# Duplicate key halves made on ScalarE and GpSimd, the weight sums of the output product issued earlier, score rows of over 512 keys in two adjoining PSUM banks, in a one-core encoder layer

## The chip, the core and the metric

The kernel runs on one core of a Trainium2 chip. The core has a matrix engine (TensorE: PE for its matmuls, PEld for loading the stationary operand), VectorE (DVE), ScalarE (ACT), GpSimd (POOL) and a sync engine (SP) whose queue issues every transfer of this kernel. Matmuls write to PSUM, eight banks of 512 fp32 columns on 128 partitions; all other tiles are in SBUF. The engines run side by side, each works through its own queue in order, and they wait for one another by semaphores. The metric is the device time of one launch in microseconds (us).

## What is computed

One layer for 1024 prompt positions and 32 sample positions of 1024 features. Everything is fp32; for accuracy each operand of a matmul is split into a rounded high part and a low remainder (`h` and `l` in tile names), and two or three products are summed.

```python
u = rmsnorm(h, g_pre) @ w_in                 # w_in (1024, 4096)
qa, ka, va, ga, qb, kb, vb, gb = split(u)    # 512 columns each, 8 heads x 64
oA = band_attention(qa, ka, va, rel_bias)    # softmax, own 64-frame chunk and the 8 before
oB = stick_breaking(qb, kb, vb)              # strictly causal
y  = concat(oA * silu(ga), oB * silu(gb)) @ w_out
h  = h + rmsnorm(y, g_post)
h  = h + sigmoid(h @ w_ple_gate) * (p @ w_ple)

def stick_breaking(q, k, v, q_pos, k_pos):
    z = einsum(q, k) * ATTN_SCALE
    causal = k_pos < q_pos
    log_beta = log_sigmoid(z)
    log_1m = where(causal, log_sigmoid(-z), 0.0)
    after = reverse_cumsum(log_1m) - log_1m
    w = where(causal, exp(log_beta + after), 0.0)
    return einsum(w, v)
```

The keys and values are outputs as well, and so is the same layer for the sample rows, which attend to caches of 512 earlier positions.

## The kernel before

The program first records all operations with what each reads and writes; `Recorder.order` then lays out the five queues by the hand-kept table of numbers `ORDER` (numbers of recorded operations, one list per engine). `Recorder.emit` issues them from one line, so every instruction of the profile stands at L502, and is told apart by its tiles' names.

**Stages.** In the first 25 us the rows of `x` are loaded, squared on ACT, scaled on DVE (`be<-om,ms,gpre`) and turned on the PE in pieces of 128x128 (`ptx`); ACT writes the high part `hnh` and DVE the low part `hnl`. The matmuls `gpre` spread the norm's weights over the partitions, and the product of `p` and `w_ple` for half of the rows (`ptp`, `php`, `ple`) is made there too. Then the first three column groups of `w_in` are projected (`mm_kA`, `mm_qA`, `mm_vA`, three chunks of 352 rows, 24 matmuls each). After that eight pairs of heads, A and B in turn, go through the attention while `weave` puts the projections of the next pair between their steps; the weights of `w_in` are loaded in halves `wr`, and ACT and POOL split them into `wh` and `wl`. From about 560 us on the output product (`o0P` to `o3P`) and the gate product (`g0P` to `g3P`) run by a scheme of seven products of half-size blocks, which needs sums and differences of the weights' quarters.

**Attention.** `prep_k` makes for each head the high part `kd` (ACT) and the low part `kl` (POOL) of the keys on its 64 partitions, and copies both to the other 64 partitions by a transfer (`kd<-kd`, `kl<-kl`). `scores(i)` makes one row block of 128 queries. Block i sees i+1 blocks of 128 keys, in a band head (A) at most five. With up to 512 keys it takes one PSUM tile with the tag `S`; with more it is cut in two halves, each with a tile, its two matmuls, and its own operations after that: in a B head a sigmoid on ACT and a running product on DVE (`om<-om,SB`), in an A head the custom operation that adds the bias and keeps the running minimum (`om<-SA,biasA`, with a short read of `statA`). POOL then takes differences (B), ACT exponentials (A). The weights are turned (`STREAM_TRANSPOSE`, transfers `swap`, or for the last B rows on the PE, `ptwB`) and split into `wTh` and `wTl`, and `values` multiplies them with the values (`PVA`, `PVB`).

**PSUM.** The banks are given by tags: two for projections, three for `S`, two for turned tiles (`T`), one for `PV`. A tile with a tag waits until all readers of the one that had the bank have ended. `S` also serves `gpre`, and the products of the output stage; `T` also `ptp`, `ptx`, `ptk` (keys of the caches), and in the output stage the copy in PSUM (named `x` and the operand, as in `xS4o`) of each left operand, out of which DVE takes the low part.

**Weight sums.** `sum_weights(w, kt)` loads four quarters (`oB` or `gB`, 256 KB each), makes four sums on POOL in eight instructions, and stores four results. There are four `kt` for the output weights (`o`) and four for the gate's (`g`); `with_sums` puts the eight calls into the attention of pairs 0, 0, 1, 1 (`o`) and 4, 4, 5, 5 (`g`).

Of the kernel before, what the change touches and what calls it, by code (L numbers as in the profile page):

```python
# [13 lines left out]
P = 128  # L14
D = 1024
SEQ = 1024
# [28 lines left out]
0-11 14 12 15 13 16 19-21 18 22-23 17 48-51 26 24 27 25 57 56 54 60 52 61-63 29-30 53 31 28 55 59 66 33-34 32 67 35 58 64-65 37 39 38 36 68 70-71 42-43 41 69 40  # L45
72-77 90-91 45 47 46 44 78-79 92 80-83 93-95 97 99 98 96 120-122 101 100 102-103 123-127 144-149 128-129 106-107 105 130-136 104 109 108 110-111 137-143 150-158
117-118 116 119 168-170 159 114-115 113 112 171-189 199 197 190 198 196 84 160 194 193 192 195 85-86 191 161-167 87 204-205 207 206 88-89 202 200 203 216-222
240-263 201 223-230 214 212 215 213 231-232 210-211 208-209 233-239 288-294 264-287 295-359 362 360 368 370 363-367 372-373 361 369 371 374-376 378-379 392-395
377 380-382 408-409 396 410-411 383 438-439 397-403 384-386 440-441 456-457 387 454-455 388-391 404-407 412-417 426-437 442-453 458-469 472-477 480-491 508-510
470 478 526 511-513 471 479 527 514-517 534-535 550-551 548-549 518-521 558-559 522 560-561 523-524 594-597 525 528-532 610-611 533 536-541 418-425 612-613  # L50
542-547 552-557 562-573 582-583 492-495 584-593 598 496-507 599-600 626-627 601-609 614-625 634-635 628-630 636 676-677 631-633 574-581 637-647 664 690-691 665
698-699 666-669 700-701 670-675 678-682 708-709 683-689 692-697 702-705 744-745 706-707 712-713 710-711 648-651 714-722 652-663 760-761 723 746-747 732-743
748-759 764-767 778-779 768 776-777 769-774 762-763 775 780 724-731 781-783 786-791 800-802 828-835 840-841 854-855 836-839 784-785 842-845 803-805 822-827
846-853 856-861 872-873 862 792-799 863-871 876-887 806-809 896-899 810-821 874-875 908-909 900-907 912-923 928 924-925 929-931 910-911 932-939 942-947 950-952
888-891 953-955 964-966 940-941 967-969 986-987 926-927 988-997 892-895 998-1003 1006-1017 1020-1031 1036-1037 1004-1005 1018-1019 1038-1040 948-949 1041-1046
1032-1033 1047 1034-1035 1052-1053 1048-1049 957 956 958-959 963 960-962 1050-1051 1054-1063 1072 970-973 1073-1076 1108 1077 974-981 1080 982-985 1081
1114-1115 1078-1079 1082-1087 1096-1098 1116-1117 1099-1101 1064-1067 1102-1103 1093 1089 1095 1068-1070 1091 1094 1088 1071 1090 1092 1130-1131 1104 1109-1113
1105-1107 1118-1124 1150-1161 1174-1175 1162-1171 1125-1129 1144-1149 1133 1135 1132 1134 1136 1138 1140 1137 1142 1139 1141 1143 1176-1177 1255 1222-1223 1256
1230-1231 1178-1181 1257-1258 1273-1274 1182-1183 1271-1272 1184 1172-1173 1185-1187 1334-1335 1204-1205 1188-1191 1336-1337 1206-1207 1192-1195 1350-1351
1196-1203 1208-1221 1224-1227 1249 1238-1242 1228 1250 1229 1232 1251-1254 1233-1237 1243-1248 1259 1287 1260-1262 1288 1263-1264 1289-1292 1281-1283 1265  # L60
1352-1353 1266-1268 1293 1269-1270 1275-1280 1284 1294-1296 1430 1297-1299 1374-1375 1382 1431 1300-1301 1383 1285-1286 1302-1313 1322-1323 1328-1332 1438-1439
1333 1452-1453 1338-1339 1324-1325 1454-1455 1326-1327 1340-1349 1354-1359 1462-1463 1360-1361 1314-1320 1367 1321 1366 1362-1365 1368-1373 1376-1378 1390-1395
1412-1429 1379-1381 1384-1386 1492-1493 1387-1389 1464-1471 1480-1481 1432-1437 1440-1446 1396-1399 1447-1450 1516-1517 1451 1456-1458 1494-1495 1459-1460
1400-1411 1461 1482-1491 1504-1506 1532-1533 1507 1472-1479 1518-1519 1497 1496 1498-1499 1501-1502 1500 1503 1508-1515 1520-1531 1546-1548 1552-1554 1549-1551
1564-1565 1555-1558 1602 1559-1560 1603-1606 1561-1563 1566-1569 1607-1608 1573 1572 1574 1535 1537 1577-1578 1534 1536 1575 1579 1576 1570-1571 1580-1585
1609-1613 1539 1541 1543 1545 1538 1540 1542 1544 1635 1641 1586-1589 1614 1636 1615 1590-1592 1628 1593 1629 1594-1596 1620-1621 1597-1601 1634 1632-1633 1631
1630 1642 1616-1619 1622-1625 1657-1658 1626-1627 1637-1640 1643-1645 1667-1668 1646-1648 1669-1672 1649-1656 1673 1661-1666 1682-1687 1708-1709 1718-1719
1688-1689 1659-1660 1690 1674-1681 1691-1693 1702-1704 1740 1705-1707 1712 1724-1725 1741 1713-1715 1710-1711 1716-1717 1720-1722 1694-1697 1723 1728-1730
1698-1700 1731 1760-1761 1742-1743 1762 1701 1763-1767 1726-1727 1768-1771 1732-1739 1744-1749 1788-1793 1802-1803 1794-1799 1804-1813 1816 1832-1833 1817-1821
1826-1830 1834 1831 1835 1814 1800 1815 1801 1836-1837 1842 1750-1751 1872 1843-1846 1873-1874 1847-1848 1838-1839 1822-1825 1754-1756 1753 1752 1759 1758 1757  # L70
1849 1840-1841 1850 1870-1871 1851 1868-1869 1852 1884 1772-1775 1853 1862 1885 1875 1776-1787 1886-1887 1863-1864 1876-1880 1900-1901 1881-1883 1865-1867
1888-1899 1902-1913 1916-1917 1944-1947 1918 1914-1915 1919-1922 1948 1854-1857 1923-1927 1949 1956-1957 1970-1971 1978-1979 1950-1955 1980 1858-1861 1981
1994-1995 1958-1966 1996-1997 1967-1969 1972-1977 1982 2024-2025 1983-1993 1998-2008 2026-2027 2009 2042-2043 2018 2040-2041 2019-2023 2028-2035 2062-2063
2036-2039 2044-2050 1928-1931 2051-2054 2072 2055-2058 2070-2071 2059 2073-2080 1932-1943 2112 2140 2113 2141 2126-2127 2081-2083 2100-2111 2060-2061 2064-2069
2142-2148 2114 2156-2157 2115-2116 2010-2017 2117-2122 2149-2153 2123 2192-2193 2124-2125 2128 2158-2159 2129-2133 2154-2155 2160-2165 2084-2087 2166-2171
2134-2139 2208-2209 2212 2088-2094 2194-2195 2095-2099 2213 2180-2189 2214 2190-2191 2196-2197 2215-2217 2236-2237 2218-2223 2210-2211 2224 2198-2204 2172-2178
2205-2206 2225 2207 2226-2227 2179 2228-2231 2238-2240 2232-2235 2241-2243 2318 2326-2327 2319 2244-2245 2288 2250-2251 2246 2289 2247-2249 2260 2290-2301 2257
2252 2255 2253 2259 2254 2258 2256 2302-2305 2340-2341 2306-2310 2356-2357 2311 2261-2263 2342-2343 2264-2271 2344-2351 2272-2275 2352-2355 2360-2362 2276-2281
2392 2282-2285 2393 2358-2359 2286-2287 2363-2370 2312-2315 2371 2316-2317 2320-2325 2328-2332 2408-2409 2333-2335 2394-2395 2336-2339 2412-2419 2372-2375
2380-2381 2420-2421 2382 2422-2426 2383 2436-2437 2384-2389 2410-2411 2376-2379 2390-2391 2396-2407 2427-2435 2438-2448 2526 2512-2513 2527 2449 2460-2461  # L80
2450-2451 2462-2466 2536 2544-2545 2534 2537 2535 2467-2468 2459 2453-2454 2456 2452 2457-2458 2455 2469-2471 2488 2546-2547 2489-2494 2576 2495-2496 2574-2575
2497 2604-2605 2498-2502 2472-2475 2503-2508 2476-2479 2577 2480 2606-2607 2481-2487 2620-2621 2514-2519 2509-2511 2520-2525 2528-2533 2538-2543 2560-2563 2548
2584 2588 2585-2587 2589 2591 2590 2564-2567 2549-2558 2592-2603 2608-2611 2652-2653 2612-2619 2559 2568-2573 2578-2583 2676-2680 2622 2624 2623 2625 2681 2627
2629 2631 2626 2633 2628 2630 2632 2682-2685 2634-2637 2694-2695 2638-2651 2721 2723 2702 2660 2703 2661-2667 2722 2668-2669 2731-2732 2724 2670 2733-2734
2671-2675 2706 2704-2705 2708 2707 2654-2656 2788-2789 2657 2790-2791 2658-2659 2686-2688 2804-2805 2689-2692 2709-2714 2747 2715 2748-2752 2716-2717 2693
2696-2698 2753 2699-2701 2754-2758 2718-2720 2725-2726 2806-2807 2727-2730 2735-2746 2762-2773 2782-2787 2792-2801 2824-2828 2802-2803 2808-2811 2759 2830-2831
2816-2817 2866-2867 2812-2813 2818 2760-2761 2819-2823 2829 2832-2837 2815 2774-2781 2900-2901 2880-2881 2902-2903 2854-2858 2814 2859-2865 2868-2871 2916-2917
# [420 lines left out]
def stream_step(  # L508
# [16 lines left out]
    def psum(tag, name):  # L525
        return ps.tile([P, 512], F32, tag=tag, name=name, bufs=PS_BUFS[tag])

# [925 lines left out]
    for c in range(NCH):  # L1453
# [3 lines left out]
        for j in range(3):  # L1457
            for st in first[j][PARTS * c:PARTS * (c + 1)]:
                st[1]()
# [493 lines left out]
```

## Time and profile before

| | |
|---|---|
| three runs | 774.55, 769.46, 771.27 us; median 771.27 us |
| the profiled execution | 768.86 us, of which the span from the first to the last instruction is 767.1 us |
| granted PE clock, mean over the span | 0.999 |
| PE, PEld busy | 749.7 us, 684.7 us |
| DVE, ACT, POOL busy | 600.3, 497.1, 483.7 us |
| moved by DMA | 192.70 MB |

In the profile "busy" is the time in which an engine has at least one instruction under way. A PE matmul is in flight for longer than it takes up the array, so that neighbours overlap. "<-" in a wait is followed by what ended it; a tile's name without its number stands for all its buffers.

### The profile page before, as it was taken

What the parts mean: (1) busy time and instruction counts of PE and PEld (TensorE: products, weight loads), DVE (VectorE), ACT (ScalarE), POOL (GpSimd) and SP (SyncE); (2) the same over time, 40 slices, a digit from 0 to 9 for tenths busy, and PEclk for the clock granted to TensorE, in tenths of its full rate; (3) what the DMA queues carried; (4) which work ended last, traced back from release to release, by engine and by line L of the source; (5) the groups of instructions that cost most, each with busy time, mean ns of one, the idle gap of its engine ahead of it and who ended that gap; (6) DMA issues with size and microseconds to landing.
All of it is one profiled execution on the core that took longest, in us unless ns stands there. A gap on an engine that the chain in (4) does not pass through costs nothing.

```text
span 767.1 us, 13431 instructions
## 1 busy us (share of the span) xinstructions
PE 749.7 (98%) x4262; PEld 684.7 (89%) x4262; DVE 600.3 (78%) x961; ACT 497.1 (65%) x985; POOL 483.7 (63%) x589
## 2 busy tenths in 40 slices
PE   7999999999999999999999999999999999999997
PEld 6999999999989999899998999999997877888786
DVE  6825799989788988898988978979555669686665
ACT  4726686657787555777746857565238977775641
POOL 5705386974564857367697334768751869999533
PEclk9999999999999999999999999999999999999999
DMA  9418999989999867999999899786679959879844
GB/s 312 135 37 236 286 271 284 271 237 269 302 265 265 259 153 238 270 263 279 290 282 294 251 231 273 216 270 198 195 264 314 344 179 332 290 264 352 294 145 137
DMA packets 194040, 192.70 MB, mean 251 GB/s; under 512 B 43201, under 2 KB 148713, under 8 KB 193970
## 3 DMA queue, kind: packets, MB, share of 16 engines
q1 hardware_dynamic: 193970, 191.86, 83.0%
q8 instruction: 33, 0.54, 0.3%
q14 instruction: 37, 0.30, 0.1%
HBM read 107.62 MB, written 65.30 MB: 225 GB/s over the span
## 4 chain that ended last, share of the span: by engine, by line
PE 76%; DMA 9%; DVE 7%; ACT 4%; issue 3%; SPq 1%; DVEq 0%; ACTq 0%
PE mm_gA L502 6%; PE mm_vA L502 6%; PE mm_qA L502 5%; PE mm_kA L502 5%; PE mm_kB L502 4%; PE SB L502 4%; PE mm_gB L502 4%; PE PVB L502 4%; DVE om L502 3%; PE o3P L502 3%; PE g1P L502 3%; PE o1P L502 3%; PE g0P L502 3%; PE g2P L502 3%; PE o0P L502 3%
## 5 line engine op out<-in xcount | busy, mean ns | idle before, releaser
L502 DVE TENSOR_TENSOR wTl<-be,wTh 128x640 fp32r<-128x640 f32 (+4 forms) x104 | 96.1, 944 | 9.2 <-ACT wTh L502 8.6
L502 POOL TENSOR_TENSOR be<-om 128x128 f32<-128x128 f32 (+7 forms) x64 | 80.0, 1255 | 27.4 <-DVE om L502 11.7
L502 DVE TENSOR_TENSOR_SCAN om<-om,SB 128x512 f32<-128x512 f32 (+5 forms) x96 | 93.8, 995 | 4.2 <-POOL om L502 3.3
L502 ACT CAST wTh<-be 128x640 fp32r<-128x640 f32 (+4 forms) x104 | 66.8, 669 | 25.5 <-DMA be<-om 9.7
L502 DVE STREAM_TRANSPOSE om<-be 128x640 f32<-128x640 f32 (+3 forms) x72 | 73.5, 1026 | 12.0 <-ACT be L502 6.4
L502 ACT ACTIVATE om<-SB 128x384 f32<-128x384 f32 (+5 forms) x96 | 45.1, 493 | 20.2 <-PE SB L502 18.0
L502 ACT ACTIVATE be<-om,statA 128x640 f32<-128x640 f32 (+3 forms) x64 | 47.1, 744 | 10.8 <-DVE wTl L502 8.1
L502 POOL TENSOR_SCALAR_AFFINE_SELECT om<-om 128x128 f32<-128x128 f32 x64 | 25.8, 410 | 23.8 <-ACT om L502 22.2
L502 POOL TENSOR_TENSOR gB<-gB,gB 128x256 f32<-128x256 f32 x32 | 24.8, 798 | 20.4 <-DMA gB<-in_w_ple_gate_dram 20.3
L502 POOL TENSOR_TENSOR oB<-oB,oB 128x256 f32<-128x256 f32 x32 | 26.0, 830 | 16.3 <-DMA oB<-in_w_out_dram 13.0
L502 DVE CUSTOM_DVE_ANT_0 om<-SA,biasA 128x320 f32<-128x320 f32 (+4 forms) x64 | 29.5, 484 | 7.7 <-PE SA L502 2.4
L502 PE MATMUL SB<-kdB,LB 128*128 128x384 f32 (+5 forms) x96 | 33.6, 357 | 0.4 <-DVE om L502 0.4
L502 PE MATMUL SB<-klB,LB 128*128 128x384 f32 (+5 forms) x96 | 32.4, 344 | 0.0
L502 PE MATMUL SA<-kdA,LA 128*128 128x320 f32 (+3 forms) x96 | 29.3, 324 | 1.8 <-DVE statA L502 1.8
L502 POOL TENSOR_TENSOR klB<-stkB,kdB 64x1024 fp32r<-64x1024 f32 x8 | 19.5, 2442 | 16.6 <-DMA oB<-in_w_out_dram 9.8
L502 PE MATMUL SA<-klA,LA 128*128 128x320 f32 (+3 forms) x96 | 28.6, 316 | 0.1
L502 POOL TENSOR_TENSOR sggA<-sggA,oggA 128x352 f32<-128x352 f32 x24 | 23.9, 1002 | 1.5 <-DMA oggA<-rs_dr 0.7
L502 POOL TENSOR_TENSOR sggB<-sggB,oggB 128x352 f32<-128x352 f32 x12 | 12.7, 1059 | 18.1 <-DMA oggB<-o_dr 6.5
L502 POOL TENSOR_TENSOR klA<-stkA,kdA 64x1024 fp32r<-64x1024 f32 x8 | 20.8, 2598 | 4.9 <-DMA ple_dr<-pleo 4.5
L502 POOL TENSOR_TENSOR h<-h,x 128x512 f32<-128x512 f32 (+1 forms) x18 | 23.1, 1301 | 0.3 <-DVE h L502 0.2
L502 PE MATMUL PVB<-wTl,v2B 128*128 128x512 f32 (+1 forms) x96 | 22.2, 344 | 0.0
L502 PE MATMUL PVB<-wTh,v2B 128*128 128x512 f32 (+1 forms) x96 | 21.6, 342 | 0.1
(679 smaller groups left out, 2532.1 us busy)
## 6 DMA issues: line engine op xcount, KB each, us to landing
be<-om SPq DMA_DIRECT2D x64, 160.0 KB
swapA<-om SPq DMA_DIRECT2D x32, 320.0 KB
be<-swapA SPq DMA_DIRECT2D x32, 320.0 KB
oB<-in_w_out_dram SPq DMA_DIRECT2D x16, 256.0 KB
sum_dro<-oB SPq DMA_DIRECT2D x16, 256.0 KB
gB<-in_w_ple_gate_dram SPq DMA_DIRECT2D x16, 256.0 KB
sum_drg<-gB SPq DMA_DIRECT2D x16, 256.0 KB
x<-in_x_prompt_dram SPq DMA_DIRECT2D x16, 256.0 KB
```

The costliest lines, as they stand in the source:

```text
L502: getattr(getattr(tc.nc, o.what[0]), o.what[1])(*args, **kw)
```

## The change

Three edits in the code, and a new table.

- `prep_k`: the two transfers are gone. ACT copies the keys a second time, to the other 64 partitions, and POOL copies `kl` there.
- PSUM: the four banks of `S` are now one ring from which a tile of 512 or of 1024 columns is cut, and `T` has one bank. A row block with more than 512 keys takes a tile of 1024 columns and lies around its middle, so that each half of the matmuls stays in its bank, and the operations after that take the whole row in one instruction. In the profile of the changed kernel all tiles of the ring have the name `S`.
- `sum_weights` for `o` is called in the first projection stage, after half of the steps of the column groups 1, 3, 5 and 7 of nine (chunk by chunk, three groups in each). The four calls for `g` go to pairs 0, 2, 4 and 6.

```diff
-    PS_BUFS = {"mm": 2, "S": 3, "T": 2, "PV": 1}
+    PS_BUFS = {"mm": 2, "T": 1, "PV": 1}
+    BANKS = 4
 
     def psum(tag, name):
+        if tag not in PS_BUFS:
+            return sring.tile([P, 512], name)
         return ps.tile([P, 512], F32, tag=tag, name=name, bufs=PS_BUFS[tag])
+
+    sring = Arena(rec, ps, "S", BANKS * 512)
...
         nc.scalar.copy(kd[r], st[r, 0:SEQ])
+        nc.scalar.copy(kd[o], st[r, 0:SEQ])
         nc.gpsimd.tensor_tensor(kl[r], st[r, 0:SEQ], f(kd[r]), ALU.subtract)
-        dma(f(kd[o]), f(kd[r]))
-        dma(f(kl[o]), f(kl[r]))
+        nc.gpsimd.tensor_copy(kl[o], f(kl[r]))
...
+            if n > 512:
+                wide = sring.tile([P, 1024], f"S{nm}_{i}")[:, 512 - n // 2:512 + n // 2]
+            else:
+                wide = psum("S", f"S{nm}_{i}")[:, 0:n]
             for j in range(len(cut) - 1):
-                s = psum("S", f"S{nm}_{i}_{j}")[:, 0:cut[j + 1] - cut[j]]
+                s = wide[:, cut[j]:cut[j + 1]]
...
-                pieces.append((cut[j], cut[j + 1], s))
+            pieces.append((0, n, wide))
...
-    SUMS_AT = (0, 0, 1, 1, 4, 4, 5, 5)
+    SUMS_EARLY = (1, 3, 5, 7)
+    SUMS_AT = (0, 2, 4, 6)
...
+                if i == PARTS // 2 and (3 * c + j) in SUMS_EARLY:
+                    sum_weights("o", kt)
+                    kt += 1
...
-            att = with_sums(att, [("og"[i // 4], i % 4) for i in range(8) if SUMS_AT[i] == n])
+            att = with_sums(att, [("g", i) for i in range(4) if SUMS_AT[i] == n])
```

The table `ORDER` is new for all five engines; two of its lines:

```diff
-6 0 5 1-3 9 4 7 14 8 10-12 15 13 33 18 21 31 22 30 16 19 17 20 23 50 28 51 29 49 79 32 39 77 34 78 38 35 41 40 26 42 24 44 25 45 27 97-98 61 63 62 60 65 36 68
+1 3 5 0 2 6-7 4 8 14 9-11 13 12 15 18 63 29 64-65 62 16 30 17 28 27 78-79 20 19 31 60 22 21 23-24 32 25 61 77 105 33 26 35 34 70 67 66 68-69 104 103 56-58 36 73
```

**The first transfers on SP.** Before (`om` and `x` are tiles of the input rows, `pp` the input `p`, `wpr` its weights, `grow` the norm's weights):

```order
L502 DMA om<-in_x_prompt_dram 128x1024
L502 DMA grow<-in_g_pre_dram 1x1024
L502 DMA om<-in_x_prompt_dram 128x1024
L502 DMA pp_222<-in_p_prompt_dram 128x2x256 x2
L502 DMA wpr_0True<-in_w_ple_dram 128x512
L502 DMA om<-in_x_prompt_dram 128x1024
```

After:

```order
L497 DMA pp_222<-in_p_prompt_dram 128x2x256
L497 DMA wpr_0True<-in_w_ple_dram 128x512
L497 DMA om<-in_x_prompt_dram 128x1024
L497 DMA grow<-in_g_pre_dram 1x1024
L497 DMA pp_222<-in_p_prompt_dram 128x2x256
L497 DMA om<-in_x_prompt_dram 128x1024
```

The first half of `p` moved from fourth place to first and its weights to second; the row tile that stood first is sixth.

**The low parts of the first pair's keys on POOL** (`klA`, two heads; `wl` are low parts of projection weights, `ksS` and `qsS` columns for the sample rows). Before:

```order
L502 TENSOR_TENSOR klA_674<-stkA_271,kdA_649 64x1024
L502 TENSOR_SCALAR ksS<-stkA_271 128x32
L502 TENSOR_TENSOR wl_qB_1_890<-wr_qB_1_561,wh_qB_1_889 128x512
L502 TENSOR_TENSOR wl_qB_0_872<-wr_qB_0_530,wh_qB_0_871 128x512
L502 TENSOR_SCALAR qsS<-stqA_460 128x32
L502 TENSOR_TENSOR klA_923<-stkA_271,kdA_886 64x1024
```

After:

```order
L497 TENSOR_TENSOR klA_447<-stkA_266,kdA_446 64x1024
L497 CAST klA_447<-klA_447 64x1024
L497 TENSOR_TENSOR wl_qB_1_913<-wr_qB_1_554,wh_qB_1_912 128x512
L497 TENSOR_SCALAR ksS<-stkA_266 128x32
L497 TENSOR_TENSOR wl_qB_0_898<-wr_qB_0_524,wh_qB_0_897 128x512
L497 TENSOR_SCALAR qsS<-stqA_465 128x32
L497 TENSOR_TENSOR oB_691<-oB_691,oB_744 128x256 x2
L497 TENSOR_TENSOR oB_744<-oB_734,oB_744 128x256 x2
L497 TENSOR_TENSOR klA_910<-stkA_266,kdA_909 64x1024
L497 CAST klA_910<-klA_910 64x1024
```

Behind each difference stands the copy, and four instructions of the sums `oB` now stand ahead of the second head's.

**Turned tiles of the input on the PE in the first projections** (`ptx`; `mm_kA` and `mm_qA` are projections). Before:

```order
L502 MATMUL ptx_0_507<-ident,be 128x128 x3
L502 MATMUL mm_kA_0_459<-hnh_176,wl_kA_0_207 128x352 x2
L502 MATMUL mm_kA_0_459<-hnh_176,wl_kA_1_230 128x352 x4
L502 MATMUL mm_kA_0_459<-hnl_179,wh_kA_0_206 128x352
L502 MATMUL ptx_0_507<-ident,be 128x128
L502 MATMUL ptx_1_529<-ident,be 128x128 x4
```

After:

```order
L497 MATMUL ptx_0_488<-ident,be 128x128 x4
L497 MATMUL mm_kA_0_444<-hnh_176,wl_kA_0_207 128x352
L497 MATMUL mm_qA_0_466<-hnh_176,wh_qA_1_291 128x352 x3
L497 MATMUL mm_qA_0_466<-hnh_176,wl_qA_0_265 128x352 x2
L497 MATMUL mm_kA_0_444<-hnh_176,wl_kA_0_207 128x352
L497 MATMUL mm_kA_0_444<-hnh_176,wl_kA_1_228 128x352 x4
L497 MATMUL mm_qA_0_466<-hnh_176,wl_qA_0_265 128x352
L497 MATMUL ptx_1_523<-ident,be 128x128 x4
```

Where two tiles followed each other, twelve projection matmuls now stand between them.

More of the change, by code (lines that the diff above doesn't have):

```diff
@@ L49 @@
[L49 to L56, printed above, removed]
@@ new lines @@
+1336 1334-1335 1337 1167-1168 1352 1350-1351 1353 1169-1173 1188-1203 1249-1251 1216 1252-1254 1259-1260 1217-1219 1238-1239 1241 1240 1220-1221 1261-1270
+1275-1280 1224-1225 1287 1226-1228 1242 1229 1232-1237 1243-1248 1288-1292 1328-1329 1374 1382 1375 1383 1330-1331 1438 1430-1431 1439 1293 1332 1281 1333
+1338-1339 1282-1285 1294-1299 1286 1302-1305 1454-1455 1452-1453 1306-1313 1300 1322-1327 1340-1348 1462-1465 1349 1354-1363 1301 1364-1365 1368-1373 1376-1381
+1384-1385 1366 1314 1367 1315-1321 1386-1395 1412-1415 1518-1519 1516-1517 1416-1419 1494-1495 1492 1420-1425 1432-1434 1426-1427 1493 1396-1399 1428 1400-1407
@@ new lines @@
+1429 1408-1410 1435-1437 1440-1443 1411 1444-1450 1466-1470 1451 1471 1480 1499 1496 1498 1497 1456-1457 1481-1483 1458-1461 1484-1486 1532-1533 1487-1491
+1504-1507 1510-1513 1564-1565 1514-1515 1508-1509 1520-1526 1620-1621 1527 1472-1479 1500-1503 1528-1531 1546-1563 1566-1571 1580-1582 1572-1575 1583-1584
+1602-1613 1578 1576 1579 1577 1535 1534 1536-1537 1586-1591 1538-1539 1541 1543 1540 1545 1542 1592 1544 1593-1601 1641-1644 1585 1628-1629 1614-1619 1635-1636
+1630-1633 1622-1627 1637-1640 1645-1647 1708-1711 1648-1649 1682 1657-1660 1667-1668 1650-1652 1634 1669-1672 1653-1656 1661-1666 1683-1689 1724-1725 1673
@@ new lines @@
+1726-1727 1674-1681 1690-1693 1702-1705 1741 1740 1706-1707 1712-1723 1728-1733 1694-1697 1734-1737 1760 1742-1743 1750-1751 1738-1739 1744-1749 1761-1771
+1788-1795 1698-1701 1796-1799 1802-1813 1816-1818 1832-1837 1842-1847 1819-1821 1826-1831 1848-1853 1872 1862-1863 1822-1825 1864-1867 1873-1883 1888 1800-1801
+1814-1815 1889-1898 1870-1871 1753 1755 1838-1841 1754 1868-1869 1752 1902 1899 1903-1907 1886-1887 1884-1885 1908-1913 1916-1923 1900-1901 1914-1915 1924
+1772-1775 1756-1759 1776-1779 1925-1927 1944-1948 1780-1787 1949-1953 1978 1980-1981 1979 1954-1955 1972-1977 1982-1988 1958-1969 1989-1991 1956 1970 1854-1857
@@ new lines @@
+1957 1971 1858-1861 1992-1993 2024-2027 1998-2006 1994-1997 2007-2009 2018-2023 2028-2039 2044-2049 2040-2043 2050-2061 2064-2065 2072 2062-2063 2070 2066-2069
+2071 2073-2080 1928-1931 2081-2083 2100-2103 2112-2113 2126-2127 2104-2105 1932-1943 2106-2111 2114-2125 2128-2133 2140-2143 2134-2139 2144-2152 2156-2159
+2010-2017 2153-2155 2160-2171 2180-2205 2212 2208 2206-2207 2213-2214 2210 2215-2217 2084-2094 2211 2095-2096 2209 2097-2099 2218-2235 2238-2241 2236-2237
+2250-2251 2242-2249 2260-2263 2172-2179 2264-2271 2288-2292 2318 2326-2327 2319 2293-2298 2340 2342-2343 2341 2252-2255 2299-2317 2320 2358 2356-2357 2359 2344
@@ new lines @@
+708 721 713 717 714 712 720 715-716 727 722-724 719 737 726 734 731 730 738 729 725 733 745 732 741 728 735-736 750 739 749 743 740 758 754 742 762-763 752 744
+771 767 747 746 776 748 772 751 780 753 756 760 788 755 784 757 765 785 759 769 761 800 774 801 766 804 770 775 778 782 768 764 787 777 773 779 797 786 781 798
+783 790 789 799 812 808 805-806 813 807 802-803 817 791 793-794 811 792 795-796 816 820 814-815 823 809-810 822 821 819 827 818 826 831-832 825 824 835 829 828
+837 834 833 838 840 830 843 841 836 845 844 839 847 846 842 849 848 851 850 852-859
@@ new lines @@
+74 83 79 51-54 77-78 96 93 97 94 56 95 168 55 104-105 58 57 102 101 59-60 166-167 103 62 61 106 112 117 109 107 110 113 108 118 111 64 114 120-121 119 115
+123-124 116 63 125 122 126-127 187 65-66 132 140 143 146 141 128-129 133 130 67 138 68 131 144 152 149 134 147 142 150 145 139 148 153 136 151 154 69-70 137
+158-159 71-72 157 160-162 156 164 85 163 165 86 135 87-88 170 169 90 89 155 92 179 91 185-186 180 183-184 171-172 189 173-176 269 181-182 188 190-191 195
+177-178 209 199 202 214 200 203 215 210 267-268 192 283 201 196 284 204 193 211 216 221 220 194 217-218 285 219 212 223 222 224 227 197 228 213 198 225 230 240
@@ L181 @@
+696 695 720 708 721 706 757 722 691 724 719 725 723 726-727 760 728-730 758 761 731-732 735 733 736 738 734 739 741-743 737 744 740 747-748 745 749-750 746
+751-756 759 762-765
 """,
@@ L1452, in stream_step @@
     first = [col_steps(j) for j in range(3)]
+    kt = 0
     for c in range(NCH):
@@ L1457, in stream_step @@
         for j in range(3):
-            for st in first[j][PARTS * c:PARTS * (c + 1)]:
+            for i, st in enumerate(first[j][PARTS * c:PARTS * (c + 1)]):
                 st[1]()
+                if i == PARTS // 2 and (3 * c + j) in SUMS_EARLY:
+                    sum_weights("o", kt)
+                    kt += 1
     for x in ple.later:
```

216 lines of the change are left out of this document (96 added, 120 removed).

## Prediction, made before the changed kernel had run

> **What bounds the kernel now.** I read the busy times and slices of the page first, then the PE's own list of waits, then busy times by stage.
>
> ```profile
> PE 749.7 (98%) x4262; PEld 684.7 (89%) x4262; DVE 600.3 (78%) x961; ACT 497.1 (65%) x985; POOL 483.7 (63%) x589
> PE   7999999999999999999999999999999999999997
> DMA  9418999989999867999999899786679959879844
> ```
>
> The PE is busy in every slice but parts of the first and last. The change removes no matmul, so it can only shorten what the PE waits for. Those waits (engine and what it was to make, what ended the wait: total us, times, longest):
>
> ```profile
> PE ptp L502 <- DMA pp<-in_p_prompt_dram: 4.0, 1, 4.0
> PE mm_gB L502 <- DVE sggB L502: 1.8, 2, 0.9
> PE SA L502 <- DVE statA L502: 1.8, 3, 0.9
> PE mm_qB L502 <- ACT stkB L502: 1.3, 1, 1.3
> PE SsB L502 <- DVE QsB L502: 0.7, 1, 0.7
> PE SB L502 <- DVE om L502: 0.4, 2, 0.2
> ```
>
> Behind the start, the five rows from `mm_gB` on sum to 6.0 us, 0.8% of the run. By stage (us: PE, PEld, DVE, ACT and POOL busy, then granted clock, DMA share, GB/s):
>
> ```profile
> 40.00:60.00 20.00, 20.00 (x129) 19.23 (x128) 3.44 (x8) 5.67 (x14) 1.39 (x6) 1.00 0.12 35
> 150.00:200.00 50.00, 50.00 (x310) 47.81 (x309) 44.16 (x76) 34.49 (x67) 31.39 (x38) 1.00 0.87 258
> 300.00:350.00 50.00, 47.38 (x292) 45.41 (x291) 44.95 (x85) 39.07 (x76) 27.97 (x32) 1.00 0.98 274
> 600.00:650.00 50.00, 50.00 (x219) 39.04 (x218) 38.81 (x66) 40.38 (x88) 41.85 (x45) 1.00 0.81 271
> ```
>
> From 150 to 200 us and from 600 to 650 us the PE has no gap at all, though the DMA queues (0.87) and DVE (44.16 of 50) are heavily loaded: their load is mostly hidden. So the start is the largest single piece.
>
> **The first transfers (new order on SP).** The start in the chain of work that ended last (start, us, what), four rows of the timeline (start, us, engine), and two stretches:
>
> ```profile
> 1.94 6.12 DMA pp<-in_p_prompt_dram
> 8.19 1.53 PE ptp L502 x6
> 11.85 1.71 PE ple L502 x4
> 23.05 2.33 PE ple L502 x10
> ...
> 0.72 0.39 SPq L502 DMA_DIRECT2D om<-in_x_prompt_dram  x1
> 3.96 1.06 ACT L502 ACTIVATE be<-om 128x1024 f32<-128x1024 f32 x1 [1.96 <-DMA om<-in_x_prompt_dram]
> 9.31 0.59 ACT L502 CAST php<-ptp 128x512 fp32r<-128x512 f32 x1 [1.82 <-PE ptp L502]
> 25.57 0.73 PE L502 MATMUL mm_kA<-hnh,wh_kA 128*128 128x352 f32 x3
> ...
> 4.30:8.19 3.89, 0.00 (x1) 0.03 (x1) 1.82 (x2) 1.96 (x4) 2.15 (x4) 1.00 0.90 296
> 8.19:13.80 5.61, 5.61 (x19) 4.36 (x20) 3.81 (x6) 3.02 (x6) 1.74 (x3) 1.00 1.05 380
> ```
>
> The PE idles from 4.30 to 8.19 us for `pp`, and then runs at half rate: four `ple` matmuls take 1.71 us (428 ns each), later ten take 2.33 (233 each). The 19 instructions of 8.19 to 13.80 us would take half of 5.61, 2.8 us, at the later rate; so of the first 13.8 us 11.0 are lost. Now `pp`'s first half goes first. The first 512 KB transfer, issued at 0.72 us, had landed by 3.96; half as much should be there by then, and the PE can start at about 4.3, when its warming matmuls end. It must then wait for the high parts of `p` and of the weights on ACT (two operations like the `php` row's 0.59 us, some 1.3 with the hand-over). Lost are 4.3 + 1.3 + another 2.8 for a half-rate stretch of the same length = 8.4 us, a gain of 2.6; without that stretch 5.6, a gain of 5.4. Against it: the row tiles come later (the first of them drops to sixth), which could take all of it. Ends 0 and -5.4; I take -3.5, nearer the middle since the later stretch to 50 us shows a PE without a wait, work enough to move forward. (Between the granted clock of 1.00 in these rows and the doubled matmul time I believe the matmul time.)
>
> The Trainium skill, TensorE: Matmul & The Clock Gate, section What's actually happening, says that the PE drops to half rate after an idle window of about 3.4 us and returns after as long a busy one. The 3.89 us gap followed by 428 ns matmuls agrees; by that rule a start at 4.3 us keeps what the warming matmuls have gained, and the gain would be the larger one of the two.
>
> **Duplicate key halves.** 32 transfers of 256 KB go, 8.4 of 192.7 MB; 16 copies on ACT and 16 on POOL come. Prices (mean ns behind the bar, or min/median/max):
>
> ```profile
> L502 ACT CAST kdA<-stkA 64x1024 fp32r<-64x1024 f32 x8 | 8.4, 1050 | 5.3 <-PE SB L502 5.2
> L502 POOL CAST wTl<-wr_vA x2: 612/612/612, 29.0 to 31.8; 128x512 fp32r<-128x512 f32 x2
> L502 DVE TENSOR_TENSOR wTl<-be,wTh x104: 258/825/3394, 82.5 to 557.7; 128x640 fp32r<-128x640 f32 x40, 128x896 fp32r<-128x896 f32 x24, 128x256 fp32r<-128x256 f32 x16, 128x128 fp32r<-128x128 f32 x16
> 323.41 2.39 POOL L502 TENSOR_TENSOR klB<-stkB,kdB 64x1024 fp32r<-64x1024 f32 x1
> 323.93 3.39 DVE L502 TENSOR_TENSOR wTl<-be,wTh 128x256 fp32r<-128x256 f32 x1
> 325.76 1.27 POOL L502 TENSOR_TENSOR wl_vB<-wr_vB,wh_vB 128x512 fp32r<-128x512 f32 x1
> 327.84 0.44 PE L502 MATMUL SA<-kdA,LA 128*128 128x384 f32 x1 [0.86 <-DVE statA L502]
> ```
>
> ACT: 16 x 1.05 = +16.8 us; POOL: twice the columns of a 0.61 us copy, 16 x 1.22 = +19.5 us. Both engines are busy for two thirds of the span, so most is covered; no PE wait names a `kd` or `kl` transfer, so the transfers' end is worth 0 on the path. But a POOL instruction can stretch a DVE one: `wTl` at 323.93 took 3.39 us instead of 0.8, right while `klB` and `wl_vB` ran on POOL, and the PE's `SA` matmul behind it waited 0.86. The copy prolongs just such a run of POOL work. Ends: 0, and 16 x 1.22 = 19.5 us if each copy reaches the PE so. One of 16 differences did here in full; I take +1.
>
> The Trainium skill, SBUF — State Buffer, section Who interferes with whom, states that a DVE instruction with two SBUF inputs and a GpSimd one that reads SBUF exclude each other for a whole instruction. The three rows at 323 to 327 us agree. By that rule alone the sum would be what the last rival below gives.
>
> **Wide score rows.** 32 sigmoids, 32 running products and 32 bias operations are merged into their neighbours. Fixed costs from two sizes each:
>
> ```profile
> L502 ACT ACTIVATE om<-SB 128x512 f32<-128x512 f32 x24 | 14.4, 601 | 4.2 <-PE SB L502 4.0
> L502 ACT ACTIVATE om<-SB 128x256 f32<-128x256 f32 x8 | 3.1, 385 | 0.3 <-PE SB L502 0.3
> L502 DVE TENSOR_TENSOR_SCAN om<-om,SB 128x512 f32<-128x512 f32 x24 | 30.3, 1263 | 1.3 <-POOL om L502 1.1
> L502 DVE TENSOR_TENSOR_SCAN om<-om,SB 128x384 f32<-128x384 f32 x24 | 23.9, 998 | 0.4 <-POOL om L502 0.2
> ```
>
> Sigmoid: 216 ns for 256 columns, so 0.17 us is fixed: 32 x 0.17 = -5.4 us of ACT. Running product: 265 ns for 128 columns, 0.20 fixed: -6.4 us of DVE, and, by my estimate, about as much for the bias operation. Neither engine is the bound, so these are worth 0 themselves. What reaches the path is the bank count: the PE's waits for `S` banks are 1.8 + 0.4 = 2.2 us, and four banks instead of three let it run one bank further ahead, though a wide tile frees its two only together. One of the waits is the `wTl` story above. Ends 0 and -2.2; I take -1.5.
>
> **Sums.** The sums of `o` on POOL (ns min/median/max, first and last start):
>
> ```profile
> L502 POOL TENSOR_TENSOR oB<-oB,oB x32: 723/743/1668, 101.6 to 226.4; 128x256 f32<-128x256 f32 x32
> ```
>
> Sixteen loads and sixteen stores for `o` (8.4 MB) and 23.8 us of POOL work (32 x 0.743 us) leave 101 to 226 us for the first projections, where from 40 to 60 us the DMA share is 0.12 and POOL is busy for 1.39 of 20. The PE lost next to nothing in the old place, so this is 0; in the new one loads on SP wait for PE and buffers with the sample rows' load queued behind them, needed only by the ninth tile: 0 to +2, I take 0. The `g` sums no longer come in twos: around them lie `mm_gB`, `mm_qB` and `SsB`, 3.8 us of waits. Ends 0 and -3.8; I take -1, the new order having its own late comers.
>
> **One `T` bank.** A turned or copied tile must be emptied before the next is begun:
>
> ```profile
> 616.35 0.60 ACT L502 COPY xS4o<-uo 128x512 f32<-128x512 f32 x1
> 616.98 0.69 DVE L502 TENSOR_TENSOR S4o<-xS4o,S4o 128x512 fp32r<-128x512 f32 x1 [0.43 <-ACT xS4o L502]
> 618.65 0.61 ACT L502 COPY xA11o<-uo 128x512 f32<-128x512 f32 x1
> 624.11 0.68 DVE L502 TENSOR_TENSOR A11o<-xA11o,A11o 128x512 fp32r<-128x512 f32 x1
> 602.80 2.76 PE o0P L502 x12
> ```
>
> Emptying takes 1.3 us (616.35 to 617.67) when DVE comes at once, and took 6.1 when it did not; one operand is needed per 2.76 us product. With the order laid out anew for one bank, 1.3 to 2 fits, also between the input's tiles, where twelve projection matmuls now stand. Ends 0 and 2 sets x 14 x (3.7 - 2.76) = 26 us, 3.7 being the mean of 1.3 and 6.1; I take +0.5, since two rows of slack in operands stand before every product.
>
> **Sum.** -3.5 + 1 - 1.5 + 0 - 1 + 0.5 = -4.5 us on the profiled execution's 768.86 us, 764.4. That execution lies 2.4 us below the median of the three runs, 771.27, and on the median I forecast 771.27 - 4.5 = 766.8, 767 us.
>
> **Rivals.**
> - All of it comes: the full 5.4 at the start, all 6.0 us of later waits: 771.3 - 11.4 = 760 us. For: each wait has its own small cause, and DVE loses 13 us of work. Against: a new order of five queues has new late comers.
> - Nothing comes: the gain of the start is given back, because from 300 to 350 us (PE 47.38 of 50) transfers and ACT set the pace, and the early PE only waits longer: 771 us.
> - Slower: the POOL copies shut DVE out, as `klB` and `wl_vB` did, and the PE's score matmuls wait for DVE: 19.5 - 5 = +14.5, 786 us. It decides against the change from the fifth of the 16 copies on that is met in full (5 x 1.22 us against the 5.5 saved), and passes 1% at the eleventh. Against: DVE's waits here were almost all hidden.
>
> **Chances.** The forecast (763 to 772) 0.50, all of it 0.22, nothing 0.16, slower by POOL 0.12. A measurement of this kernel tells about 1% from no change (the three runs spread over 0.7%), that is 763.6 and 779.0. Faster by more: 0.9 of the second case and a fifth of the first, 0.30; slower by more: most of the last, 0.10; within: 0.60. The range 757 to 778 leaves out most of the last case and the far end of the second.
>
> **What would show it.** Right: the first `ptp` starts at 4 to 5 us and the first `mm_kA` 2 to 5 us before its old 25.6; PE waits for score banks under 1.5 us; POOL busy about 503, ACT about 509, DVE some 13 us less; PE without gaps from 600 to 680 us. Wrong: a PE wait on `ptx` or on a left operand through `T`; a median of DVE's `wTl` well above 0.83 us with PE waits behind it; an early start that is lost again by 100 us.

## The result, and the profile after

The changed kernel takes 977.08 us (median of 4 runs, 975.6 to 983.33) where the kernel before took 772.91 in the same measurement (4 runs, 769.46 to 774.82): 1.266 times as long, 95% interval 1.259 to 1.274. The forecast was 767 us, in a range of 757 to 778. The profiled execution took 977.99 us, with a span of 976.1.

The page of the changed kernel (busy times; then the PE's and the DMA's share by slices, and between them the granted clock):

```profile
PE 813.9 (83%) x4262; PEld 718.2 (74%) x4262; DVE 587.3 (60%) x865; ACT 511.0 (52%) x969; POOL 495.6 (51%) x605
PE   8997988798898987887899978999677768677774
...
PEclk9999999799899999999999999999989898898997
DMA  7557986658866476656467858478733355386332
```

The work is roughly as announced: DVE loses 13.0 us, ACT gains 13.9 and POOL 11.9 (for POOL some 19 had been expected). But the PE, which was busy in almost every slice, now has gaps everywhere. Of the 209.0 us by which the span grew (976.1 - 767.1), 144.8 are idle PE (976.1 - 813.9 = 162.2, where it was 767.1 - 749.7 = 17.4) and 64.2 are busy PE, though the matmuls are the same 4262.

What the PE waits for in the changed kernel (tile it was to write, what ended the wait: total us, times, longest), the first five rows and one more:

```profile
PE S L497 <- DVE om L497: 40.8, 22, 4.3
PE S L497 <- DVE h L497: 28.3, 16, 3.9
PE S L497 <- DVE statA L497: 23.7, 17, 4.3
PE S L497 <- DVE uu L497: 11.1, 6, 3.8
PE S L497 <- ACT ple L497: 7.5, 5, 3.8
...
PE ptp L497 <- DMA pp<-in_p_prompt_dram: 0.3, 1, 0.3
```

And DVE's list, from the same profile:

```profile
DVE h L497 <- PE S L497: 57.6, 14, 8.5
DVE om L497 <- PE S L497: 44.3, 21, 7.2
DVE uu L497 <- PE S L497: 24.7, 8, 5.0
```

Nearly all of it is one tile, `S`, the ring of four banks, and it goes both ways: the PE waits for DVE's reads, and DVE waits for the PE's writes. Neither engine is short of time; they take turns. The first transfers did what was wanted (the wait for `pp` fell from 4.0 us to 0.3).

Three stretches of the changed kernel (busy us of PE, PEld, DVE, ACT, POOL with their counts, granted clock, DMA share, GB/s):

```profile
150.00:200.00 50.00, 39.63 (x198) 36.74 (x197) 30.02 (x31) 23.39 (x38) 34.53 (x41) 0.83 0.54 161
600.00:650.00 50.00, 45.78 (x270) 43.87 (x269) 33.00 (x44) 17.89 (x37) 33.54 (x40) 0.93 0.60 176
700.00:750.00 50.00, 37.21 (x133) 27.19 (x132) 19.90 (x34) 25.39 (x53) 18.53 (x15) 0.90 0.47 151
```

From 150 to 200 us the kernel before did 310 matmuls in 50.00 us of busy PE, 161 ns each on average; here 198 take 39.63, 200 ns each, at a granted clock of 0.83. The clock falls where the PE has waited. One such place, in rows of the timeline with seven matmuls of one shape each (the first and the last), and as a stretch:

```profile
481.15 1.34 PE L497 MATMUL mm_vA<-hnl,wh_vA 128*128 128x352 f32 x7
...
484.31 0.33 PE L497 MATMUL S<-kdA,LA 128*128 128x128 f32 x1 [1.66 <-DVE om L497]
...
484.99 2.26 PE L497 MATMUL mm_gB<-hnh,wh_gB 128*128 128x352 f32 x7
...
484.70:488.10 3.40, 3.40 (x14) 3.40 (x14) 0.56 (x1) 0.37 (x2) 3.40 (x3) 0.50 0.34 135
```

Behind a wait of 1.66 us the clock is at half for 3.40 us, and the seven matmuls take 2.26 us instead of 1.34. In the whole trace the clock is at half in 26 stretches, and the PE is busy in them for 101 us; neighbouring matmuls of 512 columns start 427 ns apart there, and 231 ns apart elsewhere. So by an estimate some 46 of the 64.2 us come from the clock, 101 x (1 - 231 / 427). The other 18 were not taken apart; the busy time now falls into 106 pieces instead of 16, and at the end of each a matmul has no neighbour to overlap with. The Trainium skill, TensorE: Matmul & The Clock Gate, section What's actually happening, puts the idle window that does this at about 3.4 us; the trace agrees only in part, since the longest waits in the rows above, 3.8 to 4.3 us, have that length, but the wait of 1.66 us was enough as well.

How the engines take turns shows in the output stage, in four rows of the timeline (start, us, engine, instruction, idle time before and what ended it):

```profile
746.79 0.40 PE L497 MATMUL S<-oT,wlS1o 128*128 128x512 f32 x1
...
757.85 3.84 PE L497 MATMUL S<-oB,wh8o 128*64 128x512 f32 x16
...
761.72 1.29 DVE L497 TENSOR_TENSOR h<-h,S 128x512 f32<-128x512 f32 x2 [8.53 <-PE S L497]
...
763.15 1.12 PE L497 MATMUL S<-oB,wl8o 128*64 128x512 f32 x4 [1.47 <-DVE h L497]
```

The two reads at 761.72 us read the second bank, which the product with `wlS1o` had finished at 747.2. In the built program their semaphore wait is for the last matmul with `wh8o`, which writes to the first bank and ends at 761.69: they idle 8.53 us for data that they do not read. Then the PE waits 1.47 us for them, since `wl8o` goes into the second bank, which they read.

This is the rule in the built program, not a single case. Of the 90 waits for a PE matmul into `S` which DVE and ACT instructions that read `S` carry themselves, 76 name a matmul into a bank that the instruction does not touch. And of 673 pairs of a matmul into `S` and the last DVE access ahead of it, where that is to another bank, the PE is made to wait for that access, or a later one, in all 673. A part of such waits would be there for other reasons: of 638 such pairs in the first run below (one tile, the orders of the kernel before) all are waited for, and of the same 638 in the kernel before, 228. The same class `Arena` cuts `om` out of one SBUF tile, and there not every such pair is waited for (ACT writing, DVE ahead of it in other columns): 4 of 100 in the kernel before, 38 of 66 in the changed one, where it was not taken apart how many of the 38 have other reasons. So the conjecture: **in PSUM the waits follow the whole tile and the order in which the program is written down; four banks cut from one tile are, for the waits, one buffer.**

### The profile page after: what moved, and what is told of

The parts are those of the page before. It is cut to its first block, busy times and chain, and to the rows that moved or that the text cites. A ratio compares the mean times of both kernels' runs of the same rounds, so it can differ in the third digit from the quotient of the medians.

```text
span 976.1 us, 13232 instructions
## 1 busy us (share of the span) xinstructions
PE 813.9 (83%) x4262; PEld 718.2 (74%) x4262; DVE 587.3 (60%) x865; ACT 511.0 (52%) x969; POOL 495.6 (51%) x605
## 5 line engine op out<-in xcount | busy, mean ns | idle before, releaser
L497 DVE TENSOR_TENSOR_SCAN om<-om,S 128x128 f32<-128x128 f32 (+8 forms) x68 | 91.0, 1362 | 52.6 <-issue 13.9
L497 ACT CAST wTh<-be 128x640 fp32r<-128x640 f32 (+4 forms) x104 | 66.4, 667 | 17.5 <-DMA be<-om 4.5
L497 PE MATMUL S<-kdB,LB 128*128 128x384 f32 (+5 forms) x96 | 35.8, 398 | 38.4 <-DVE om L497 35.4
L497 DVE CUSTOM_DVE_ANT_0 om<-S,biasA 128x640 f32<-128x640 f32 (+4 forms) x64 | 40.4, 649 | 44.7 <-PE S L497 35.3
L497 ACT ACTIVATE om<-S 128x896 f32<-128x896 f32 (+8 forms) x68 | 41.2, 639 | 48.7 <-PE S L497 40.7
L497 PE MATMUL S<-kdA,LA 128*128 128x320 f32 (+4 forms) x96 | 30.3, 347 | 28.4 <-DVE statA L497 20.7
L497 PEld LDWEIGHTS S<-kdB,LB 128*128 128x128 f32 x96 | 19.2, 206 | 44.9 <-DVE om L497 36.4
L497 PEld LDWEIGHTS S<-kdA,LA 128*128 128x128 f32 x96 | 17.6, 193 | 35.6 <-DVE statA L497 25.9
L497 DVE TENSOR_TENSOR h<-h,S 128x512 f32<-128x512 f32 x20 | 13.4, 684 | 43.7 <-PE S L497 43.7
L497 PE MATMUL S<-klB,LB 128*128 128x384 f32 (+4 forms) x96 | 34.0, 370 | 0.0
L497 POOL TENSOR_TENSOR sggB<-sggB,oggB 128x352 f32<-128x352 f32 x12 | 11.9, 989 | 32.8 <-DMA oggB<-o_dr 18.6
L497 PE MATMUL S<-klA,LA 128*128 128x320 f32 (+4 forms) x96 | 28.1, 320 | 0.0
```

The costliest lines, as they stand in the source:

```text
L497: getattr(getattr(tc.nc, o.what[0]), o.what[1])(*args, **kw)
```

## The experiments

The rivals: the single `T` bank, the copies on POOL, the wide operations (which hold two banks), the new order, the early sums. The first four runs take these apart.

**The kernel before with its score banks cut from one tile.** Nothing else differs, not the order, nor the banks.

```diff
-    PS_BUFS = {"mm": 2, "S": 3, "T": 2, "PV": 1}
+    PS_BUFS = {"mm": 2, "T": 2, "PV": 1}
     def psum(tag, name):
+        if tag not in PS_BUFS:
+            return sring.tile([P, 512], name)
...
+    sring = Arena(rec, ps, "S", 3 * 512)
```

> The kernel before, with its three score banks cut in turn from one PSUM tile of 1536 columns instead of three tiles of 512; the order of every queue, the two T banks and the narrow operations are those of before. Theory (the waits follow the whole tile, so that a matmul into one bank waits for the readers of the others): waits of the PE on DVE and ACT for this tile of over 80 us in all, where it was 2.2, the granted clock below 0.97, and 880 to 1010 us. Rivals (one T bank, the copies on POOL, wide operations, the new order, the early sums): none of them is in it, so 765 to 780 us.

Measured: 1013.28 us (2 runs), against 771.43 for the kernel before in the same job, ratio 1.314 (1.305 to 1.324). Its mean granted clock is 0.938, and its three largest waits sum to 100.1 us:

```profile
PE S L502 <- DVE om L502: 43.5, 23, 4.4
PE S L502 <- DVE statA L502: 34.9, 22, 6.1
PE S L502 <- DVE h L502: 21.7, 15, 3.6
```

The one tile alone makes a loss of this size, with the same rows and orders. The time lies just above what was expected (1010 was the upper end). That it is more than the changed kernel's 977 may come from three banks instead of four; no run shows it, since the two kernels differ in more.

**The changed kernel with four tiles.** The reverse: the ring is four tiles of 512 columns, so that rows of over 512 keys are read in two operations again, each second one right behind its first.

```diff
-    PS_BUFS = {"mm": 2, "T": 1, "PV": 1}
-    BANKS = 4
+    PS_BUFS = {"mm": 2, "S": 4, "T": 1, "PV": 1}
...
-                s = wide[:, cut[j]:cut[j + 1]]
+                s = psum("S", f"S{nm}_{i}_{j}")[:, 0:cut[j + 1] - cut[j]]
...
-            pieces.append((0, n, wide))
+                pieces.append((cut[j], cut[j + 1], s))
```

> The changed kernel with four separate PSUM tiles of 512 columns in place of the one of 2048, and so two operations for each row of over 512 keys again, the second right behind the first; the key copies, the early sums, the one T bank and the new order stay. Theory (the one tile): nearly all of the 204 us goes, 760 to 785 us, and waits of the PE for score banks sum to under 10 us. Rivals: if the one T bank, the copies, the early sums or the order made the loss, it stays above 900 us; if the waits for score banks hide a second loss behind them, 790 to 900 us.

Measured: 767.6 us (10 runs), ratio to before 0.9966 (0.994 to 0.9992). Its busy times, and the stretches shown above:

```profile
PE 748.1 (98%) x4262; PEld 686.9 (90%) x4262; DVE 598.0 (78%) x961; ACT 514.8 (67%) x1001; POOL 503.4 (66%) x605
```

```profile
150.00:200.00 50.00, 45.06 (x264) 42.27 (x263) 37.96 (x62) 30.34 (x59) 32.28 (x32) 0.97 0.67 197
600.00:650.00 50.00, 50.00 (x219) 39.05 (x218) 40.42 (x69) 42.07 (x92) 43.74 (x47) 1.00 0.86 275
700.00:750.00 50.00, 50.00 (x218) 38.96 (x217) 32.44 (x55) 27.85 (x54) 23.74 (x19) 1.00 0.64 220
```

All of the loss is gone with the one tile, and of the PE's waits ahead of score matmuls 0.8 us is left. The T bank, the copies, the early sums and the new order are all in this kernel, which is 0.1 to 0.6% faster than the one before: none of them carries the loss. From 150 to 200 us it still waits; that is taken up in the last experiment.

**Two tiles of two banks.** The wide operations stay.

```diff
-    sring = Arena(rec, ps, "S", BANKS * 512)
+    sring = Banks(rec, ps, "S")
```

`Banks` gives out halves of two tiles `Su` and `Sv` of 1024 columns in turn; a wide row takes a whole one.

> The changed kernel with its four score banks in two PSUM tiles of 1024 columns instead of one of 2048; a wide row takes one tile, two narrow ones share one. Theory (waits by the whole tile): matmuls wait for the reader of the neighbouring bank only, so about half of the loss or more goes, 800 to 900 us. If waits went by banks and the loss came from the wide operations' holding two banks, it stays near 977 us, 950 to 1000.

Measured: 806.47 us (2 runs), ratio 1.046 (1.042 to 1.050): 84% of the loss goes, (977.1 - 806.5) / (977.1 - 772.9). What is left lies in the output stage:

```profile
450.00:500.00 50.00, 50.00 (x312) 48.10 (x311) 44.50 (x58) 37.22 (x64) 38.45 (x46) 1.00 0.84 248
...
600.00:650.00 50.00, 43.02 (x181) 31.91 (x182) 26.01 (x46) 29.73 (x65) 26.28 (x27) 1.00 0.57 176
700.00:750.00 50.00, 45.63 (x192) 33.58 (x191) 31.61 (x56) 23.91 (x47) 33.90 (x33) 1.00 0.87 297
```

Up to 580 us, behind the attention, the two are level (two tiles with the wide operations, then four tiles with the narrow ones):

```profile
0.00:580.00 580.00, 566.83 (x3479) 544.65 (x3480) 465.32 (x653) 387.38 (x718) 375.98 (x485) 0.99 0.79 234
0.00:580.00 580.00, 569.03 (x3480) 545.85 (x3481) 468.34 (x750) 389.72 (x752) 376.61 (x485) 0.99 0.79 234
```

One has done 3479 matmuls by then and the other 3480, though DVE is busy for 3.0 us less with the wide operations. So the wide operations are not the cause of the loss, and no gain of theirs shows; since the two kernels also differ in who shares a tile, a small gain could be hidden by a small cost of that. Counted by the columns of matmul work, 75% are done by this time. The one tile reaches that after 680 us: of its 211 us (976.1 - 765.0, the spans) about 100 are lost up to there and 111 behind it.

**The copies alone**, in the kernel before:

```diff
         nc.scalar.copy(kd[r], st[r, 0:SEQ])
+        nc.scalar.copy(kd[o], st[r, 0:SEQ])
         nc.gpsimd.tensor_tensor(kl[r], st[r, 0:SEQ], f(kd[r]), ALU.subtract)
-        dma(f(kd[o]), f(kd[r]))
-        dma(f(kl[o]), f(kl[r]))
+        nc.gpsimd.tensor_copy(kl[o], f(kl[r]))
```

> The kernel before with the 32 transfers of key halves replaced by 16 copies on ACT and 16 on POOL, each right behind the operation that makes its half; all else as before. The forecast's term: +1 us, 768 to 776 us. Rival (POOL copies shut DVE out): +14 us or more, 785 us. If the copies carried the changed kernel's loss: over 900 us.

Measured: 771.5 us (10 runs), ratio 1.0002 (0.9975 to 1.0029). The copies cost nothing that can be measured, -1.9 to +2.2 us, and DVE's `wTl` is not stretched more often than before: in both kernels 16 of the 104 take over one and a half times the median of their shape (shortest, median, longest ns, all shapes together):

```profile
L511 DVE TENSOR_TENSOR wTl<-be,wTh x104: 265/825/2364, 81.9 to 559.3; 128x640 fp32r<-128x640 f32 x40, 128x896 fp32r<-128x896 f32 x24, 128x256 fp32r<-128x256 f32 x16, 128x128 fp32r<-128x128 f32 x16
```

**Does the written order matter?** The four runs leave open whether the waits really follow the order in which the program is written, or only the tile. `Recorder.order` merges the five queues into one sequence, the PE's as early as it can. Here the PE's next instruction is written only when no other engine can go on; each queue's own order is the same.

```diff
-            for e, line in lines.items():
+            for e, line in list(lines.items())[1:]:
...
+            if len(out) == n and lines["PE"][at["PE"]].after <= done:
+                out.append(lines["PE"][at["PE"]])
+                done.add(out[-1])
+                at["PE"] += 1
```

> The changed kernel with its one tile of 2048 columns; every engine's own order is the same, only the interleaving in which the five orders are written into the program differs: a matmul is written when no other engine can be taken further, instead of as early as possible. Theory (a matmul waits for all reads of the tile that stand before it in the program, whatever the bank): now the read of the last product stands before the next product, so the PE runs no bank ahead and waits more: 1020 to 1250 us. Rival (the waits are those of the banks, or come from the chip's memory): the orders of the engines and all data are the same, so 965 to 990 us.

Measured: 1033.6 us (one run), 56 more than the changed kernel, though no engine does anything in another order. So it matters. The PE's waits ahead of matmuls into `S` sum to 183 us, where they were 142, out of 192 and 152 us for all its waits. The four tiles were not run with the late writing, so what it costs without a shared tile is not shown.

**Who shares a tile?** Two tiles again, with the bank used longest ago for each narrow tile and the tile used longest ago for a wide row.

> The two tiles of two banks again, but each new narrow tile takes the bank used longest ago, in the order first tile, second tile, first, second, and a wide row the tile used longest ago. Theory (a matmul waits for readers of the whole tile): a product of the output stage now shares its tile with the product two before it, whose reader is mostly done, instead of the one before it. Of the 33 us which the two tiles lost in the output stage against four tiles (580 to 792 us against 580 to 759) under 15 stay: 765 to 785 us. Rival (two tiles cost this by the wide operations or by their number, not by who shares): it stays at 800 to 812 us.

Measured: 806.03 us (4 runs), ratio 1.0458 (1.0391 to 1.0525). The expectation was not tested: by this choice the banks came out two by two as before (`Su`, `Su`, `Sv`, `Sv`), so the run only repeats the 806.5.

Two more runs with the late writing: the two tiles as they are, and with the output products really from `Su` and `Sv` in turn.

```diff
-            lo = min((0, 2, 1, 3), key=lambda x: age[x])
+            out = name[0] in "og"
+            lo = min((0, 1, 2, 3), key=lambda x: (out and self.turn == x // 2, age[x]))
+        self.turn = lo // 2
```

> Two tiles of two banks, banks taken in the order first tile, first tile, second, second, and each matmul written into the program as late as possible (after the reads that can be written before it). Theory (a matmul waits for the reads of its whole tile that stand before it in the program): every second product shares its tile with the product just before it, whose read now stands before it, so the PE stops for that read every second time: 830 to 930 us, of which the output stage loses more than the 33 us of the two tiles written early. Rival (the writing order does not matter): 800 to 812 us.

> As the run with two tiles written late, but the products of the output stage really take their banks from the two tiles in turn (in the earlier run the oldest bank was chosen and the order came out as two by two). Theory: a product now waits for the read of the product two before it, and a read for its own product alone, so the output stage (75 to 99.9% of the matmul work) takes under 190 us, against 212 us in the run with two tiles written early and 179 with four tiles; the attention is as in the run with two tiles written late. Rival (two tiles cost this much in the output stage whoever shares): 205 us or more.

Measured: 861.39 and 845.24 us (one run each). Written late, the two tiles lose 55 us more, as expected, and the last quarter of the matmul work takes 230 us instead of 212. In turn it takes 209: less by 21, as the theory has it in sign, but not the under 190 that I expected; by the bounds set beforehand this is the rival's outcome (205 or more). So who shares a tile explains a part of it at most. Why so much is left there was not followed further.

**One transfer on SP.** In the kernel with four tiles, SP's list of waits from 140 to 160 us has one long wait for POOL:

```profile
SPq L506 <- POOL oB L506: 7.9, 1, 7.9
```

The timeline of the same kernel shows what stands behind it:

```profile
155.86 1.43 POOL L506 TENSOR_TENSOR oB<-oB,oB 128x256 f32<-128x256 f32 x2
...
157.32 0.36 SPq L506 DMA_DIRECT2D oB<-in_w_out_dram  x1
157.78 2.64 SPq L506 DMA_DIRECT2D be<-om  x4
...
163.51 0.30 ACT L506 CAST wTh<-be 128x128 fp32r<-128x128 f32 x1 [4.54 <-DMA be<-om]
...
165.99 0.56 PE L506 MATMUL PVB<-wTh,v2B 128*128 128x512 f32 x1 [3.53 <-ACT wTh L506]
```

A load for the third early sum waits for a buffer that POOL empties at 157.3 us; the attention's transfers `be<-om` stand behind it on SP, and at their end the PE waits 3.53 us. The run moves that load behind them:

```diff
-148-149 52 150 177 179 54 157 156 158 155 162 164 154
+148-149 52 150 177 179 157 156 158 155 54 162 164 154
```

> The kernel with four tiles and one transfer moved on SP: the load of the last quarter of the third early sum (oB), which waited 7.9 us for POOL at 149.4 us, goes behind the four transfers be<-om that stood behind it. Theory (this queueing, not the key copies or the T bank, takes back what the start gains): the PE's wait of 3.5 us for wTh at 162 to 166 us goes, and 761 to 766 us. Rival (the sums only move the wait to another transfer): 767 to 770 us.

Measured: 765.22 us (12 runs), ratio to before 0.991 (0.988 to 0.9939). The wait of 3.53 us is gone from the PE's list. This kernel is 0.6 to 1.2% faster than the one before. Against the four tiles without the move it gains some 0.56%, 4 us, though the two were measured in different jobs and their intervals (to 0.9939, from 0.994) only just part.

## Why the prediction was wrong, point by point

**Wide score rows: the step that failed.** The forecast said "four banks instead of three let it run one bank further ahead", with ends of 0 and -2.2 us. It took the ring as the recorder's own model takes it, where a tile waits for the readers of just its columns, and never asked what waits the built program holds for banks that share an allocation. In place of a gain of 1.5 us this step cost some 209 (977.1 - 767.6, the run with four tiles); the run with one tile of three banks shows that such a tile alone costs 242 in the kernel before (1013.3 - 771.4). The end on the bad side was missing: `S` is written by 1252 of the 4262 matmuls and read by DVE and ACT, and nothing in the forecast bounded what it costs to lose the overlap there.

The Trainium skill, Perfetto Trace Analysis, section Optimizing Tensor Performance, advises to rotate matmul groups through different PSUM banks so that emptying one overlaps the next. Both kernels rotate; the pair of 771 and 1013 us, on the same banks, shows that it helps only where the waits are kept by bank as well.

The rest of that term, fixed costs saved but worth 0, came as forecast. Two bias operations of 320 keys became one of 640 (x count | busy us, mean ns | idle before), before and after:

```profile
L502 DVE CUSTOM_DVE_ANT_0 om<-SA,biasA,statA 128x320 f32<-128x320 f32 x32 | 17.0, 537 | 0.6 <-PE SA L502 0.2
L502 DVE CUSTOM_DVE_ANT_0 om<-SA,biasA 128x320 f32<-128x320 f32 x32 | 15.1, 485 | 3.4 <-PE mm_kB L502 2.1 <-PE mm_vB L502 0.5 <-PE SA L502 0.3
```

```profile
L497 DVE CUSTOM_DVE_ANT_0 om<-S,biasA 128x640 f32<-128x640 f32 x32 | 26.0, 816 | 25.0 <-PE S L497 19.5 <-ACT be L497 4.3 <-POOL gB L497 0.6
```

537 + 485 - 816 = 206 ns, the 0.20 us that had been estimated from the running product.

**The first transfers** (-3.5): right in mechanism, and near the lower of its two gains, where nothing takes it back. In the changed kernel the first `ptp` starts at 4.03 us instead of 8.19, but the start is lost again before the first projection:

```profile
4.03 1.05 PE L497 MATMUL ptp<-ident,pp 128*128 128x128 f32 x4
...
12.94 0.74 PE L497 MATMUL S<-wph0True,php 128*128 128x512 f32 x2 [1.34 <-DVE be L497]
...
25.66 0.89 PE L497 MATMUL mm_kA<-hnh,wh_kA 128*128 128x352 f32 x4 [0.42 <-ACT hnh L497]
```

With four tiles the first `mm_kA` comes at 23.05 us, 2.5 before its old 25.57:

```profile
5.76 1.65 PE L506 MATMUL ple<-wph0True,php 128*128 128x512 f32 x3 [0.68 <-ACT php L506]
...
23.05 0.89 PE L506 MATMUL mm_kA<-hnh,wh_kA 128*128 128x352 f32 x4 [0.42 <-ACT hnh L506]
```

That is the gain of 2.6 us which the forecast gave for a start that still has its half-rate stretch: three `ple` matmuls of 512 columns take 1.65 us at 5.76 us (0.86 at 10.54), so the warming matmuls did not spare it, and the larger gain, for a start without it, did not come. To believe the matmul time was right: the trace's record of the clock begins only at 14.24 us before and at 9.27 us with four tiles, and the 1.00 ahead of that is no reading.

**Duplicate key halves** (+1, rival +14.5): measured -1.9 to +2.2 by themselves. Their work came as estimated, 19.6 us more on POOL and 17.5 on ACT in that run (503.3 and 514.6 busy) against 19.5 and 16.8. The rival fell; one stretched `wTl` was no guide to sixteen copies. (Its sum takes off 5 us, where the terms save 5.5; +14.0 would be right.)

**Sums** (`o` 0, `g` -1): the forecast named the risk, "loads on SP wait for PE and buffers", and gave it 0. The load waited 7.9 us, for POOL's sums, and what stood behind it was not the sample rows' load but the attention's transfers; taking it out of their way is worth about 4 us, by the two jobs above. The term was mis-sized. The `g` sums were not tried apart.

**One `T` bank** (+0.5): no wait for a turned tile is among the longer waits of the kernel with four tiles. A run with two `T` banks and all else new was not tried, so its price stays unmeasured within that kernel's -4.6 to -0.6 us.

**The sum** (-4.5) against the kernel with four tiles: -2.6 us (0.34% of 771.43, interval -4.6 to -0.6). So the other terms held in their sum, which lies just inside that interval, though not each was measured by itself; the error that counts was one term, and that it was given no bad end.

## What to carry to other kernels

Banks that should be free of one another need allocations of their own, until the built program shows otherwise: its waits can be read before any run, and here 76 of 90 named the wrong bank. An allocation that works for pieces in SBUF proves nothing for PSUM. Where a change touches the buffer through which the bounding engine hands on its work, the range needs an end for losing that overlap altogether, and a merged operation that saves time on an engine off the path is no reason to touch it.

## What the runs showed of the hardware

That waits cost more than their length: of the 209.0 us some 46, by the estimate above, were matmuls at a lower granted clock, and a wait of 1.66 us was enough for a stretch of 3.40 us at half. And that 3.0 us less of busy DVE, with the PE busy for 98% of that time, did not bring the attention forward: 3479 matmuls were done after 580 us with it and 3480 without.
